# A bidirectional recurrent scan on one Trainium2 core: conditioning blocks, their PSUM bank, chunk tiles and squares moved

## Chip, cores and metric

The kernel runs on one core of one Trainium2 chip. The metric is the time of one execution on the device, in microseconds (us). The core has TensorE (matrix products), VectorE, ScalarE and GpSimd (element-wise work) and SyncE (here it only issues DMAs). In the rows they are called PE (PEld for its weight loads), DVE, ACT, POOL and SP. Each engine runs its own instructions in order.

## What is computed

One inference step of a trunk with two layers over 128 context tokens and 512 latent tokens of width 1024. Layer 0 mixes tokens by a delta-rule recurrence in both directions (16 heads of 64), layer 1 by neighbourhood attention; a squared-ReLU MLP of width 4096 follows each. Every sub-layer is modulated by shift, scale and gate from the conditioning vector (adaLN).

```python
def ada_mod(cond, w, b):
    m = jax.nn.silu(cond) @ w + b
    return jnp.split(m, 6, axis=-1)

def delta_rule_scan(r, w, k, v, kk, a, s0, reverse):
    def step(S, inp):
        r_t, w_t, k_t, v_t, kk_t, a_t = inp
        sa = jnp.einsum('bhvk,bhk->bhv', S, -kk_t)
        S_new = (S * w_t[:, :, None, :] + sa[..., None] * (kk_t * a_t)[:, :, None, :]
                 + v_t[..., None] * k_t[:, :, None, :]).astype(S.dtype)
        y = jnp.einsum('bhvk,bhk->bhv', S_new, r_t)
        return S_new, y
...
    y = (ys[0] + ys[1]).astype(jnp.float32)
    mean = jnp.mean(y, axis=-1, keepdims=True)
    var = jnp.mean(jnp.square(y - mean), axis=-1, keepdims=True)
    yn = ((y - mean) * lax.rsqrt(var + GN_EPS)).reshape(B, T, D) * ln_w + ln_b
```

## The kernel before

The stages follow one another: projections of layer 0 (to about 290 us), the values' product and the first preparations of the scan (to 400), the scan (400 to about 760), its output product (to about 875), the MLP of layer 0 (to 1347), layer 1's attention (to about 1715) and its MLP (to the end).

The recurrence is run in chunks of 32 tokens. A scan step n (five of them) takes one tile of 128 tokens in each direction d, and has four chunk steps e = 0 to 3. `chain_step` is one chunk in one direction: the product R of the state (tile GU) with the chunk tile C; its copy Rc by ScalarE; the product U with the inverse triangle TT; four copies of U back into GU by ScalarE (L1052); `state_update`, which makes the next state in the banks G (B in the rows) with work of VectorE (L1106, L1111) or ScalarE (L1108); and the output Y, evacuated by a ScalarE copy (L1069) or, where the other direction has been there, by a VectorE sum (L1067). R, U and Y of direction d use one PSUM bank, called A, in turn (one bank for each direction).

The chunk tiles of step n+1 are prepared beside the chunks of step n, in units of half a head group: GpSimd multiplies the loaded values into C and KB (`prep_elem`, L932, L933, L947), TensorE makes the products pp (`prep_group`), ScalarE copies the triangles to invA (L972) and the rest to C (L974), VectorE masks two parts of C (L977). A pp tile lies in one of two banks that take turns. Two units are prepared per chunk step. After the last unit of a step VectorE inverts 32 x 32 triangles by forward substitution (`invert`, L984 to L998; L993 and L996 are its 100 small operations), which gives the next TT.

Finished rows of Y go through `post_half` (head norm, gate): centring (L1139), the square (L1140, ScalarE), the variance (L1142, VectorE), on GpSimd or VectorE.

adaLN of a layer is 24 blocks of 256 columns. `ada_first` loads two pieces of 512 KB (adaraw, SyncE) and makes 8 products for 16 records on TensorE (L286; under the scan's `mm` L852), ScalarE copies the sums (L289). `ada_second` makes 2 products (4 records) with the copied sums (adasb), and VectorE adds the bias into mods (L300). Layer 0's blocks 8 to 23 run in the scan, one per chunk step of steps 0 to 3, with the second stage in U's bank of direction 1. Layer 1's 24 blocks run one at a time beside the weight products of the MLP of layer 0 (8), the attention layer (12) and the MLP of layer 1 (4).

In the scan TensorE's order is the order of the program text (`mm` ties each product to the one before). On the other engines a scheduler sets the order when the kernel is built, from its own estimate of times, with the marked copies first; at run time each engine keeps that order and waits.

Of the kernel before, what the change touches and what calls it, by code (L numbers as in the profile page):

```python
# [8 lines left out]
F32 = mybir.dt.float32  # L9
F32R = mybir.dt.float32r  # L10
I32 = mybir.dt.int32
AF = mybir.ActivationFunctionType
ALU = mybir.AluOpType
# [159 lines left out]
class K:  # L173
# [243 lines left out]

    def rest_begin(self, st):
        self.sqp = self.pool(st, "sqp", 2)
        self.ada1 = list(range(24))  # L420

    def pool(self, st, name, bufs, **k):
        return st.enter_context(self.tc.tile_pool(name=name, bufs=bufs, reuse_waits="tile", **k))
# [303 lines left out]

    def c_slots(self, pool, n, par):

        for i in range(n):  # L730
            c = pool.tile([P, 26, 64], F32, name=f"C{i}")
            self.nc.any.tensor_copy(c[:, 16:18, :].rearrange("p a x -> p (a x)"), self.cst("ident"))
            self.free[par].append(c)

    def scan_pools(self, st):
# [36 lines left out]

    def phase_scan(self, st):
        nc, tc = self.nc, self.tc
        if True:
            pool = lambda name, bufs, **k: self.pool(st, name, bufs, **k)
            self.yp = pool("yp", 4)
            adp = pool("adp", 2)
            one = pool("one", 1)
            self.ch = pool("ch", 1, space=PSUM)  # L780
            self.post = pool("post", 2)
            self.G = [self.ch.tile([P, 512], F32, name=f"B{d}").rearrange("p (a b v) -> p a b v", a=2, b=4) for d in range(2)]
            self.lnwb = one.tile([P, 2, 256], F32, name="lnwb")
            nc.scalar.dma_start(self.lnwb, self.A["lnwb"].rearrange("p (a x) -> p a x", a=2))
            self.cst2 = st.enter_context(ExitStack())
            self.c_slots(self.pool(self.cst2, "c2", 1), 4, 1)
            for d in range(2):
                self.gu[d].append(one.tile([P, 2, 2, 4, 64], F32, name=f"GU{d}1"))
                for h in range(2):
                    nc.gpsimd.memset(self.gu[d][1][64 - 64 * h:96 - 64 * h, h], 0.0)  # L790
            self.gi = [0, 0]
            self.yt = {}
            self.ydone = {}
            todo, running = [], []
            ada = [(0, b) for b in range(8, 24)]

            def ada_next():
                if ada:
                    pa = self.pp_tile()
                    pa = pa[:, :256]  # L800
                    self.ada_sums.append(self.ada_first(*ada.pop(0), adp, pa, self.mm))

            self.ada_sums = []
            done = {(0, 3): [(4, 0), (4, 1)], (3, 1): [(2, 0), (1, 1)], (3, 3): [(2, 1), (1, 0)],
                    (4, 1): [(3, 0), (0, 1)], (4, 3): [(3, 1), (0, 0)]}
            pend = None
            self.pin = True
            for n, ts in enumerate(self.steps):
                for e in range(4):
                    s0, s1 = (self.chain_step(ts, n, e, d) for d in range(2))  # L810
                    next(s0)
                    if pend:
                        for x in pend:
                            next(x)
                        if n == 4 and not self.late:
                            self.late_pools()
                        for t in done.get((n, e - 1) if e else (n - 1, 3), []):
                            todo.append(self.post_half(*t, n == 4 and t[0] % 3))
                    f = (0, 1, 1, 2)
                    k = self.fill(f[0])  # L820
                    next(s0)
                    k += self.fill(f[1])
                    ada_next()
                    k += self.fill(f[2])
                    next(s1)
                    next(s0)
                    next(s0)
                    next(s1)
                    k = self.fill(f[3])
                    if k:  # L830
                        next(s1)
                    pend = [s1] if k else [s1, s1]
                    for x in running:
                        next(x)
                    m = 2 if n == 4 else 1
                    running, todo = todo[:m], todo[m:]
                    for _ in range(2):
                        for x in running:
                            next(x)
            for x in pend:  # L840
                next(x)
            for x in running:
                next(x)
            todo += [self.post_half(*t, i) for i, t in enumerate(done[4, 3])]
            for _ in range(3):
                for x in todo:
                    next(x)
            self.wo_first(adp)

    def mm(self, *a, op=None, **k):  # L850
# [49 lines left out]
    def prep_elem(self, ts, hg, d, i):  # L900
# [32 lines left out]
                nc.gpsimd.tensor_tensor(rev(KB[:, :, :, 0]), v4(dd, 1, x), f_b, op=ALU.mult)  # L933
        f_at, f_rt = (ex(w, ww), inc(w, ww)) if d == 0 else (inc(wi, ww), ex(wi, ww))
        C = ts["C"][d, hg, ww] = self.free[ts["par"]].pop(0)
        for h in range(2):
            z = C[64 - 64 * h:P - 64 * h, 8 * h:8 * h + 8, :]
            if h:
                nc.scalar.activation(z.rearrange("p a b -> p (a b)"), self.cst("scan1")[64 - 64 * h:P - 64 * h, :512],
                                     AF.Copy, scale=0.0)  # L940
            else:
                nc.gpsimd.memset(z, 0.0)
        for s, f in ((0, f_at), (1, f_rt)):
            for h in range(2):
                hs = slice(64 * h, 64 * h + 64)
# [3 lines left out]
    def prep_group(self, ts, hg, d, i, e):  # L949

        nc = self.nc
        ww = (i, 1 - i)[d]
        KB, C = ts["KB", hg, d, i], ts["C"][d, hg, ww]
        if e == 0:
            self.pa = self.pp_tile()
        pa = self.pa
        pv = pa.rearrange("p (e q x) -> p e q x", e=2, q=4)
        for q in range(4):
            for h in range(2):
                n = 8 * h + 4 * e + q  # L960
                r = 64 - 64 * h
                self.mm(pv[r:r + 64, e, q, :], lhsT=KB[:, q, e].rearrange("p s t -> p (s t)"), rhs=C[:, n:17 + h:16 + h - n, :],
                        start=True, stop=True, tile_position=(0, r))
        if e == 0:
            return
        if "D" not in ts:
            ts["D"] = self.inv.tile([P, 2, 8, 2, 32], F32, name="invA")
        mask = self.cst(f"amask{d}").unsqueeze(1).broadcast_to([P, 8, 64])
        pn = pa.rearrange("p (n x) -> p n x", x=P)
        for h in range(2):  # L970
            for b in range(2):
                nc.scalar.copy(ts["D"][32 * (2 * h + b):32 * (2 * h + b) + 32, d, 4 * hg + 2 * ww:4 * hg + 2 * ww + 2],  # L972
                               pv[64 - 64 * h:96 - 64 * h, :, b:4:2, 0:32])
        nc.scalar.copy(C[:, 18:26, :], pn[:, :, 64:P])  # L974
        for h in range(2):
            o = slice(64 - 64 * h, P - 64 * h)
            nc.vector.tensor_tensor(C[o, 8 * h:8 * h + 8, :], pn[o, :, 0:64], mask[o], op=ALU.mult)  # L977
# [23 lines left out]
    def chain_step(self, ts, n, e, d):  # L1001
# [19 lines left out]
        C = [ts["C"][d, hg, ww] for hg in range(2)]  # L1021

        def state_product(s):
            ps = self.ch.tile([P, 512], F32, name=f"A{d}")[:, :256]
            for ph, pp, hp in idx:
                q = 2 * hp + pp
                i = 8 * hp + 4 * ee + 2 * (ph % 2) + pp
                self.mm(ps[32 * q:32 * q + 32, 64 * ph:64 * ph + 64], lhsT=C[ph // 2][:, i, 32 * s:32 * s + 32],
                        rhs=gu[:, hp, pp, ph, :], start=True, stop=True, tile_position=(0, 32 * q))
            return ps  # L1030

        R = state_product(0)
        with tc.high_priority():
            Rc = self.yp.tile([P, 256], F32, name="Rc", bufs=2)
            nc.scalar.copy(Rc, R)
        yield
        TT = ts["TT"]
        ut = self.ch.tile([P, 512], F32, name=f"A{d}")
        U = ut[:, :256]
        for ph, pp, hp in idx:  # L1040
            q = 2 * hp + pp
            o = slice(64 * ph, 64 * ph + 64)
            qs = slice(32 * q, 32 * q + 32)
            self.mm(U[qs, o], lhsT=TT[qs, d * 16 + ((ph // 2) * 4 + cq) * 2 + ph % 2, :],
                    rhs=Rc[qs, o], start=True, stop=True, tile_position=(32 * q, 32 * q))
        if self.ada_sums and d == 1:
            self.ada_second(*self.ada_sums.pop(0), ut[:, 256:260], self.mm)
        with tc.high_priority():
            for pp in range(2):
                for hp in range(2):  # L1050
# [5 lines left out]
            self.state_update(ts, n, e, d, gu, nx, C)  # L1056
        self.gi[d] += 1
        yield
        Y = state_product(1)
        tt = ts["tiles"][d]  # L1060
        with tc.high_priority():
            if tt not in self.yt:
# [5 lines left out]
            else:  # L1068
                nc.scalar.copy(yo, Y)  # L1069
                self.ydone[tt].add(cq)  # L1070
        if e % 2 == 1:
            self.free[ts["par"]] += [ts["C"].pop((d, hg, ww)) for hg in range(2)]
        yield

    def state_update(self, ts, n, e, d, gu, nx, C):
# [13 lines left out]
        for pp in range(2):  # L1089
            for ph in range(4):  # L1090
                for hp in range(2):
                    i = 18 + 4 * ee + 2 * (ph % 2) + pp
                    self.mm(G[hs(hp), pp, ph, :], lhsT=C[ph // 2][ho(hp), i, :], rhs=gu[ho(hp), hp, pp, ph, :],
                            start=False, stop=True, tile_position=(64 - 64 * hp, 64 * hp), skip_group_check=True)
        FC = ts["FC"]
# [18 lines left out]
    def post_half(self, tt, hb, on_dve):  # L1114
# [22 lines left out]
        nc.vector.tensor_scalar(sm, sm, 1.0 / 64, None, op0=ALU.mult)  # L1137
        bcast = lambda a: a.unsqueeze(2).broadcast_to([P, 8, 64])
        el.tensor_tensor(Yg, Yg, bcast(sm), op=ALU.subtract)  # L1139
        nc.scalar.activation(sq, Yg, AF.Square)  # L1140
        var = po.tile([P, 8], F32, name="yvar")
        nc.vector.tensor_reduce(var, sq, axis=AX.X, op=ALU.add)  # L1142
        nc.vector.tensor_scalar(var, var, 1.0 / 64, 64e-5, op0=ALU.mult, op1=ALU.add)
# [454 lines left out]
```

## Time and profile before

| | |
|---|---|
| median of 3 runs | 2232.8 us (2231.12 to 2234.78) |
| profiled execution | 2239.71 us |
| its span on the core | 2237.9 us |
| mean granted TensorE clock | 0.944 |
| TensorE busy | 2011.6 us (90%) |
| VectorE busy | 1169.5 us (52%) |
| ScalarE busy | 857.0 us (38%) |
| GpSimd busy | 455.1 us (20%) |
| TensorE's share of the chain that ended last | 74% |
| VectorE's share of it | 13% |

The span runs from the first to the last instruction of the core. The chain that ended last is followed back from the last instruction, at each step to what released it. A busy time is the sum of an engine's instructions; short TensorE records overlap, so their durations add up to more than the time they take together.

### The profile page before, as it was taken

What the parts mean: (1) busy time and instruction counts of PE and PEld (TensorE: products, weight loads), DVE (VectorE), ACT (ScalarE), POOL (GpSimd) and SP (SyncE); (2) the same over time, 40 slices, a digit from 0 to 9 for tenths busy, and PEclk for the clock granted to TensorE, in tenths of its full rate; (3) what the DMA queues carried; (4) which work ended last, traced back from release to release, by engine and by line L of the source; (5) the groups of instructions that cost most, each with busy time, mean ns of one, the idle gap of its engine ahead of it and who ended that gap; (6) DMA issues with size and microseconds to landing.
All of it is one profiled execution on the core that took longest, in us unless ns stands there. A gap on an engine that the chain in (4) does not pass through costs nothing.

```text
span 2237.9 us, 44938 instructions
## 1 busy us (share of the span) xinstructions
PE 2011.6 (90%) x18604; PEld 1827.3 (82%) x18604; DVE 1169.5 (52%) x2592; ACT 857.0 (38%) x1712; POOL 455.1 (20%) x553
## 2 busy tenths in 40 slices
PE   6999988757665569999999999999999999999999
PEld 3777777646554568999999998889677999999999
DVE  6656658387679755433333434433666633434342
ACT  4544553546553414313131323221576331313130
POOL 0001275656542411101010110000232110101010
PEclk8997999978787788999999999999899999999999
DMA  6455764545433464323232223343310232222221
GB/s 242 147 157 155 229 205 135 173 133 166 129 132 96 112 187 141 105 76 111 72 111 76 86 76 119 132 135 92 110 57 31 75 122 76 76 76 76 76 74 69
DMA packets 161037, 260.03 MB, mean 116 GB/s; under 512 B 46528, under 2 KB 102976, under 8 KB 160832
## 3 DMA queue, kind: packets, MB, share of 16 engines
q1 hardware_dynamic: 152224, 244.05, 35.2%
q10 hardware_dynamic: 8608, 13.11, 1.7%
q8 instruction: 146, 2.39, 0.4%
q14 instruction: 59, 0.48, 0.1%
HBM read 218.18 MB, written 37.35 MB: 114 GB/s over the span
## 4 chain that ended last, share of the span: by engine, by line
PE 74%; DVE 13%; DMA 5%; POOL 3%; issue 2%; ACT 2%; SPq 1%; DVEq 0%; ACTq 0%; POOLq 0%
PE psl L205 54%; PE psl L239 3%; DVE invX L996 2%; PE ps L1525 2%; DVE invT L993 2%; POOL C L947 2%; PE po L1562 2%; PE pp L852 2%; PE pt L1550 2%; DVE C L977 1%; PE pp L1219 1%; PE psl L1265 1%; PE psl L286 1%; DMA ld_s<-scr 1%; PE A L852 1%
## 5 line engine op out<-in xcount | busy, mean ns | idle before, releaser
L191 ACT CAST whi<-wraw 128x1024 fp32r<-128x1024 f32 x178 | 186.6, 1049 | 731.5 <-PE psl L205 701.9
L205 PE MATMUL psl<-xh,whi 128*128 128x320 f32 (+1 forms) x1696 | 414.6, 317 | 9.6 <-ACT xh L247 4.9
L205 PE MATMUL psl<-xl,whi 128*128 128x320 f32 (+1 forms) x1696 | 410.2, 314 | 1.2 <-DVE xl L248 1.2
L205 PE MATMUL psl<-xh,wlo 128*128 128x320 f32 (+1 forms) x1696 | 409.7, 314 | 0.4 <-DVE ta L592 0.4
L205 PEld LDWEIGHTS psl<-xh,whi 128*128 128x128 f32 x1696 | 291.4, 191 | 28.5 <-issue 8.7
L205 PEld LDWEIGHTS psl<-xl,whi 128*128 128x128 f32 x1696 | 292.5, 191 | 5.7 <-issue 3.2
L205 PEld LDWEIGHTS psl<-xh,wlo 128*128 128x128 f32 x1696 | 292.9, 191 | 2.6 <-issue 1.7
L1172 DVE SCALAR_TENSOR_TENSOR xres<-psl,mods,xres 128x320 f32<-128x320 f32 (+2 forms) x216 | 81.7, 434 | 305.1 <-PE psl L205 305.1
L1345 POOL TENSOR_TENSOR relu<-relu 128x640 f32<-128x640 f32 x64 | 80.2, 1255 | 773.9 <-ACT relu L1344 758.7
L205 PE MATMUL psl<-hhl,whi 128*128 128x320 f32 x1024 | 233.1, 308 | 0.0
L205 PE MATMUL psl<-hhh,wlo 128*128 128x320 f32 x1024 | 233.0, 308 | 0.0
L205 PE MATMUL psl<-hhh,whi 128*128 128x320 f32 x1024 | 232.9, 308 | 0.0
L193 DVE TENSOR_TENSOR wlo<-wraw,whi 128x1024 fp32r<-128x1024 f32 x178 | 218.6, 1229 | 11.6 <-ACT whi L191 10.9
L205 PEld LDWEIGHTS psl<-hhh,whi 128*128 128x128 f32 x1024 | 170.8, 188 | 0.4 <-issue 0.4
L205 PEld LDWEIGHTS psl<-hhh,wlo 128*128 128x128 f32 x1024 | 171.1, 188 | 0.0
L205 PEld LDWEIGHTS psl<-hhl,whi 128*128 128x128 f32 x1024 | 171.0, 188 | 0.0
L1302 DVE TENSOR_TENSOR relu<-psl,rms_b 128x320 f32<-128x320 f32 x128 | 60.8, 486 | 144.6 <-PE psl L205 144.0
L852 PE MATMUL pp<-C,KB 128*64 128x128 f32 x1280 | 100.6, 306 | 39.7 <-DVE C L977 16.7
L852 PEld LDWEIGHTS pp<-C,KB 128*64 128x64 f32 x1280 | 83.0, 154 | 54.1 <-issue 28.8
L248 DVE TENSOR_TENSOR hhl<-relu,hhh 128x640 fp32r<-128x640 f32 x64 | 53.4, 834 | 127.9 <-ACT hhh L247 127.7
L1052 ACT ACTIVATE GU<-A 32x256 f32<-32x256 f32 x160 | 60.0, 375 | 93.2 <-DVE mods L300 64.0
L977 DVE TENSOR_TENSOR C<-pp,cstsb 64x512 f32<-64x512 f32 x80 | 55.0, 688 | 69.1 <-ACT C L974 56.9
(299 smaller groups left out, 3393.2 us busy)
## 6 DMA issues: line engine op xcount, KB each, us to landing
wraw<-in_mlp_w SPq DMA_DIRECT2D x128, 512.0 KB, 3.5
adaraw<-in_ada_w SPq DMA_DIRECT2D x96, 512.0 KB, 4.9
ld_d<-scr SPq DMA_DIRECT2D x20, 512.0 KB, 4.5
ld_s<-scr SPq DMA_DIRECT2D x20, 512.0 KB, 3.7
bias<-in_bias SPq DMA_DIRECT2D x16, 384.0 KB, 3.7
scr<-ta SPq DMA_DIRECT2D x16, 325.0 KB, 3.5
wi<-scr SPq DMA_DIRECT2D x20, 260.0 KB, 4.6
scr<-bp SPq DMA_DIRECT2D x16, 320.0 KB, 4.5
```

Of the source, the lines that this page charges most:

```text
L191: nc.scalar.copy(hi, raw)
L193: nc.vector.tensor_tensor(lo, raw, hi.bitcast(F32), op=ALU.subtract)
L205: self.nc.tensor.matmul(ps[g][:, :e - c], lhsT=a[:, k, :], rhs=b[:, c:e], start=(k == 0 and j == 0), stop=(k == n - 1 and j == 2))
L239: nc.tensor.matmul(ps, lhsT=a[:, tc_], rhs=w, start=(k == 0 and j == 0), stop=(k == KT - 1 and j == 2))
L248: (lo_eng or nc.vector).tensor_tensor(xl, src, xh.bitcast(F32), op=ALU.subtract)
L852: r = (op or self.nc.tensor.matmul)(*a, **k)
L947: nc.gpsimd.tensor_tensor(rev(o) if s == 0 else o, v4(sh, s, ww)[hs], f[hs], op=ALU.mult)
L977: nc.vector.tensor_tensor(C[o, 8 * h:8 * h + 8, :], pn[o, :, 0:64], mask[o], op=ALU.mult)
L1052: nc.scalar.activation(gu[64 - 64 * hp:96 - 64 * hp, hp, pp].rearrange("p b v -> p (b v)"), U[32 * q:32 * q + 32, :], AF.Copy, scale=-0.5)
L1172: nc.vector.scalar_tensor_tensor(out[:, a:b], ps[g][:, o:o + b - a], gate[:, k, j:j + 1], x[:, a:b], op0=ALU.mult, op1=ALU.add)
L1302: nc.vector.tensor_tensor(t[:, c], ps[q][:, :HALF], rb[:, c], op=ALU.mult)
L1345: nc.gpsimd.tensor_tensor(t, t, t, op=ALU.mult)
```

## The change

Four things are changed. The list of adaLN blocks that the scan works off grows by layer 1's 24; a second block is taken per chunk step in step 0 and, but for e = 1, in steps 1 to 3, which makes 29 in the scan, 13 of them layer 1's. The remaining 11 blocks of layer 1 stay with the MLP of layer 0 (8) and the attention layer (3), so that 9 leave the attention layer and 4 the MLP of layer 1. The second stage of a block goes to Y's part of the cycle: into Y's bank, behind Y's evacuation, in both directions. A chunk tile C is no longer filled with zeros; the pp products read only the 64 rows that hold values, and an identity of one slot takes the place of one of two. The square of the head norm goes from ScalarE to the engine of the centring.

```diff
@@ c_slots
-            c = pool.tile([P, 26, 64], F32, name=f"C{i}")
-            self.nc.any.tensor_copy(c[:, 16:18, :].rearrange("p a x -> p (a x)"), self.cst("ident"))
+            c = pool.tile([P, 25, 64], F32, name=f"C{i}")
+            self.nc.vector.tensor_tensor(c[:, 16], ident[:, :64], ident[:, 64:], op=ALU.add)
@@ phase_scan
+        self.ada1 = list(range(24))
-            ada = [(0, b) for b in range(8, 24)]
+            ada = [(0, b) for b in range(8, 24)] + [(1, b) for b in self.ada1]
...
                     k += self.fill(f[1])
-                    ada_next()
+                    if n < 4:
+                        ada_next()
...
                     k = self.fill(f[3])
+                    if n == 0 or n < 4 and e != 1:
+                        ada_next()
...
+            self.ada1 = [b for _, b in ada]
             self.wo_first(adp)
@@ prep_elem
-        for h in range(2):
-            z = C[64 - 64 * h:P - 64 * h, 8 * h:8 * h + 8, :]
-            if h:
-                nc.scalar.activation(z.rearrange("p a b -> p (a b)"), self.cst("scan1")[64 - 64 * h:P - 64 * h, :512],
-                                     AF.Copy, scale=0.0)
-            else:
-                nc.gpsimd.memset(z, 0.0)
@@ prep_group
-                self.mm(pv[r:r + 64, e, q, :], lhsT=KB[:, q, e].rearrange("p s t -> p (s t)"), rhs=C[:, n:17 + h:16 + h - n, :],
-                        start=True, stop=True, tile_position=(0, r))
+                hs = slice(64 * h, 64 * h + 64)
+                self.mm(pv[r:r + 64, e, q, :], lhsT=KB[hs, q, e].rearrange("p s t -> p (s t)"), rhs=C[hs, n:17:16 - n, :],
+                        start=True, stop=True, tile_position=(64 * h, r))
@@ chain_step
-        if self.ada_sums and d == 1:
-            self.ada_second(*self.ada_sums.pop(0), ut[:, 256:260], self.mm)
...
-        Y = state_product(1)
+        pa, Y = state_product(1)
...
                 nc.scalar.copy(yo, Y)
                 self.ydone[tt].add(cq)
+            if self.ada_sums:
+                self.ada_second(*self.ada_sums.pop(0), pa[:, 256:260], self.mm)
@@ post_half
-        nc.scalar.activation(sq, Yg, AF.Square)
+        el.tensor_tensor(sq, Yg, Yg, op=ALU.mult)
```

The change also moves instructions where the diff shows nothing. Three places follow, as the built kernels have them. A row reads line, operation, output<-inputs, shape, and how many like it; the line numbers of the kernel after are a few off (L976, L1064, L1105, L1110 and L997 there are L977, L1067, L1106, L1111 and L998 before). What an instruction waits for stands in brackets where it is shown.

VectorE in step 0, chunk steps 2 and 3. Before, these rows stand inside the inversion for step 1 (invT and invX are its operations):

```order
L977 TENSOR_TENSOR C_2652<-pp_4841,cstsb 64x512
L993 TENSOR_TENSOR invT_4407<-invX 128x98
L977 TENSOR_TENSOR C_2652<-pp_4841,cstsb 64x512
L996 TENSOR_TENSOR invX<-invX,invT_4406 128x15x10
L1106 TENSOR_TENSOR GU_2637<-B_3879,FC 64x512 x2
L996 TENSOR_TENSOR invX<-invX,invT_4407 128x14x7
L1067 TENSOR_TENSOR Y<-Y,A_4920 128x256
L993 TENSOR_TENSOR invT_4406<-invX 128x140
L300 TENSOR_TENSOR mods_96<-A_4938,parsb 128x4
L1111 TENSOR_TENSOR B_3879<-B_3879,FC 128x512
```

After, from the last operation of the same inversion on (L995; L997 delivers TT):

```order
L995 TENSOR_TENSOR invX<-invX,invT_4388 128x10
L997 STREAM_TRANSPOSE TT<-invX 128x32x32
L976 TENSOR_TENSOR C_2656<-pp_4735,cstsb 64x512 x2
L921 SCALAR_TENSOR_TENSOR wi<-cstsb,wi 128x520
L1064 TENSOR_TENSOR Y<-Y,A_4813 128x256
L300 TENSOR_TENSOR mods_96<-A_4813,parsb 128x4
L976 TENSOR_TENSOR C_2652<-pp_4855,cstsb 64x512 x2
L1105 TENSOR_TENSOR GU_2637<-B_3855,FC 64x512 x2
L1110 TENSOR_TENSOR B_3855<-B_3855,FC 128x512
L1064 TENSOR_TENSOR Y<-Y,A_4934 128x256
L300 TENSOR_TENSOR mods_96<-A_4934,parsb 128x4
L976 TENSOR_TENSOR C_2660<-pp_5001,cstsb 64x512 x2
```

The masks of C, the sums of Y and the additions for GU and B that stood between the inversion's operations stand behind TT; of the eight masks (L977) of the two chunk steps two are still inside.

TensorE in a chunk step of step 1. Before, from Y of direction 0 (the product A<-GU,C) over U of direction 1 (A<-Rc,TT) to the next unit's pp:

```order
L852 MATMUL A_5918<-GU_3894,C_2669 32x64 [waits PE_49]
L852 MATMUL A_5918<-GU_3894,C_2669 32x64 x7
L852 MATMUL A_5918<-GU_3894,C_3888 32x64 x8
L852 MATMUL A_5936<-Rc,TT 32x64 [waits Activation_49]
L852 MATMUL A_5936<-Rc,TT 32x64 x15
L852 MATMUL A_5936<-cstsb,adasb 128x2 x2
L852 MATMUL pp_5960<-C_3886,KB 64x128 [waits DVE_49,Pool_49]
```

After, the same stretch of a chunk step:

```order
L857 MATMUL A_6492<-GU_3870,C_2648 32x64 [waits PE_49]
L857 MATMUL A_6492<-GU_3870,C_2648 32x64 x7
L857 MATMUL A_6492<-GU_3870,C_2650 32x64 x8
L857 MATMUL A_6492<-cstsb,adasb 128x2 [waits Activation_49]
L857 MATMUL A_6492<-cstsb,adasb 128x2
L857 MATMUL A_6514<-Rc,TT 32x64 [waits PE_49]
L857 MATMUL A_6514<-Rc,TT 32x64 x15
L857 MATMUL pp_6535<-C_3864,KB 64x128 [waits DVE_49,Pool_49]
```

The second stage (cstsb,adasb) stood behind U and waited for nothing; it stands behind Y, waits for Y's copy by ScalarE, and U stands behind it.

ScalarE beside that, from the copy of R to the four copies of U of direction 1 (GU<-A). Before, in step 1:

```order
L1035 COPY Rc<-A_5881 128x256 [waits PE_49]
L1108 COPY GU_2637<-B_3879 64x512 [waits PE_49]
L1108 COPY GU_2637<-B_3879 64x512
L1069 COPY Y<-A_5918 128x256 [waits PE_49]
L917 ACTIVATE w<-wi 128x520 [waits DVE_49]
L1052 ACTIVATE GU_3897<-A_5936 32x256 [waits DVE_49]
L1052 ACTIVATE GU_3897<-A_5936 32x256 x3
```

After, at the same place of the first chunk step of step 1:

```order
L1035 COPY Rc<-A_5485 128x256 [waits PE_49,Activation_49]
L1066 COPY Y<-A_5523 128x256 [waits PE_49]
L922 ACTIVATE w<-wi 128x520 [waits DVE_49,Pool_49]
L923 ACTIVATE wi<-wi 128x520 [waits Activation_49]
L1049 ACTIVATE GU_2638<-A_5544 32x256 [waits PE_49]
L1049 ACTIVATE GU_2638<-A_5544 32x256 x3
```

The copies of U waited for VectorE, which reads the second stage out of U's bank; they wait for TensorE alone.

## Rows read from the trace of the kernel before

**Rows 1.** busy tenths of TensorE, 40 equal slices of the span (page)

```profile
PE   6999988757665569999999999999999999999999
```

**Rows 2.** by window: length; busy of PE, PEld, DVE, ACT, POOL; clock, DMA, GB/s

```profile
443.00:495.00 52.00, 25.14 (x646) 20.15 (x648) 50.99 (x138) 23.64 (x59) 29.65 (x45) 0.79 0.45 138
482.00:495.00 13.00, 0.25 (x12) 0.28 (x16) 12.85 (x44) 1.90 (x3) 6.07 (x9) 0.50 0.18 61
495.00:527.00 32.00, 28.06 (x724) 21.57 (x715) 12.93 (x26) 21.87 (x58) 18.05 (x26) 0.91 0.47 149
527.00:580.00 53.00, 30.70 (x660) 25.11 (x664) 52.29 (x139) 21.95 (x57) 33.12 (x44) 0.70 0.49 142
580.00:611.00 31.00, 27.25 (x728) 22.09 (x723) 12.12 (x18) 22.27 (x59) 14.79 (x23) 0.90 0.46 146
611.00:653.00 42.00, 24.90 (x644) 20.71 (x644) 40.42 (x120) 19.91 (x54) 23.06 (x28) 0.84 0.33 106
685.00:727.00 42.00, 22.30 (x544) 18.06 (x544) 41.41 (x148) 12.13 (x27) 11.09 (x9) 0.70 0.32 91
```

**Rows 3.** groups of instructions, VectorE, 443 to 495 us: busy us, mean ns

```profile
L996 DVE TENSOR_TENSOR invX<-invX,invT 128x108 f32<-128x108 f32 (+31 forms) x50 | 17.8, 379 | 0.3
L993 DVE TENSOR_TENSOR invT<-invX 128x20 f32<-128x20 f32 (+31 forms) x50 | 15.7, 337 | 0.3
L977 DVE TENSOR_TENSOR C<-pp,cstsb 64x512 f32<-64x512 f32 x9 | 6.2, 687 | 0.2
```

**Rows 4.** waits, 400 to 760 us: us in total, times, longest

```profile
ACT GU L1052 <- DVE mods L300: 64.0, 15, 13.2
...
PE A L852 <- DVE rsq_t L262: 19.3, 1, 19.3
...
PE A L852 <- ACT Rc L1035: 14.8, 14, 2.8
```

**Rows 5.** timeline of TensorE, 590 to 611 us: start, us, records, idle before

```profile
595.40 0.65 PE L852 MATMUL A<-Rc,TT 32*32 32x64 f32 x32 [1.11 <-ACT Rc L1035]
...
598.00 1.09 PE L852 MATMUL pp<-C,KB 128*64 128x128 f32 x16
...
599.03 0.65 PE L852 MATMUL A<-GU,C 128*32 128x64 f32 x32
...
599.61 1.15 PE L852 MATMUL B<-GU,C 64*64 64x64 f32 x32
...
609.53 0.65 PE L852 MATMUL A<-Rc,TT 32*32 32x64 f32 x32 [1.32 <-ACT Rc L1035]
```

**Rows 6.** chain that ended last, attention layer: start, us, what

```profile
1388.82 1.00 PE psl L286 x16
...
1393.92 0.54 PE psl L296 x4
```

**Rows 7.** the same chain, second MLP

```profile
1833.67 0.34 PE psl L296 x4
```

**Rows 8.** groups of instructions, all engines, 400 to 760 us

```profile
L852 PE MATMUL pp<-adaraw,condp 128*32 128x256 f32 x256 | 22.2, 470 | 3.0 <-DVE C L977 2.0 <-issue 0.8
...
L852 PE MATMUL A<-cstsb,adasb 128*128 128x2 f32 x64 | 9.7, 256 | 0.0
...
L942 POOL MEMSET C<- 64x512 f32 x28 | 14.6, 523 | 5.1 <-PE A L852 4.8
...
L1139 POOL TENSOR_TENSOR Y<-Y,ysum 128x512 f32<-128x512 f32 x5 | 5.2, 1045 | 59.1 <-DVE ysum L1137 59.0
```

**Rows 9.** chain that ended last, end of the chain stretch before 527 us

```profile
520.11 0.17 DVE mods L300
...
520.30 0.37 ACT GU L1052
...
523.52 1.23 DVE invA L984
```

**Rows 10.** the same chain, ahead of the scan, 286 to 325 us

```profile
306.37 2.86 POOL C L942 x6
```

More of the change, by code (lines that the diff above doesn't have):

```diff
@@ L419, in rest_begin @@
         self.sqp = self.pool(st, "sqp", 2)
-        self.ada1 = list(range(24))
     def pool(self, st, name, bufs, **k):
@@ L728, in c_slots @@
     def c_slots(self, pool, n, par):
+        ident = self.cst("ident")
         for i in range(n):
-            c = pool.tile([P, 26, 64], F32, name=f"C{i}")
-            self.nc.any.tensor_copy(c[:, 16:18, :].rearrange("p a x -> p (a x)"), self.cst("ident"))
+            c = pool.tile([P, 25, 64], F32, name=f"C{i}")
+            self.nc.vector.tensor_tensor(c[:, 16], ident[:, :64], ident[:, 64:], op=ALU.add)
             self.free[par].append(c)
@@ L973, in prep_group @@
                                pv[64 - 64 * h:96 - 64 * h, :, b:4:2, 0:32])
-        nc.scalar.copy(C[:, 18:26, :], pn[:, :, 64:P])
+        nc.scalar.copy(C[:, 17:25, :], pn[:, :, 64:P])
         for h in range(2):
@@ L1023, in state_product @@
         def state_product(s):
-            ps = self.ch.tile([P, 512], F32, name=f"A{d}")[:, :256]
+            pa = self.ch.tile([P, 512], F32, name=f"A{d}")
+            ps = pa[:, :256]
             for ph, pp, hp in idx:
@@ L1029, in state_product @@
                         rhs=gu[:, hp, pp, ph, :], start=True, stop=True, tile_position=(0, 32 * q))
-            return ps
-        R = state_product(0)
+            return pa, ps
+        _, R = state_product(0)
         with tc.high_priority():
@@ L1037, in chain_step @@
         TT = ts["TT"]
-        ut = self.ch.tile([P, 512], F32, name=f"A{d}")
-        U = ut[:, :256]
+        U = self.ch.tile([P, 512], F32, name=f"A{d}")[:, :256]
         for ph, pp, hp in idx:
@@ L1091, in state_update @@
                 for hp in range(2):
-                    i = 18 + 4 * ee + 2 * (ph % 2) + pp
+                    i = 17 + 4 * ee + 2 * (ph % 2) + pp
                     self.mm(G[hs(hp), pp, ph, :], lhsT=C[ph // 2][ho(hp), i, :], rhs=gu[ho(hp), hp, pp, ph, :],
```

## Prediction

> **What bounds the kernel now.** I read the busy tenths of TensorE first: full from about 840 us to the end, with a trough of fives to eights from 280 to 840 [rows 1]. In the full part a removed TensorE instruction is time saved. Most of the trough is the recurrent scan, so I cut 443 to 727 into windows at the points where VectorE's load changes [rows 2]. Two kinds of stretch alternate. In an *inversion stretch* VectorE is busy 50.99 of 52, 52.29 of 53, 40.42 of 42, 41.41 of 42 us: it solves the next step's triangles, 100 small operations (17.8 and 15.7 us of the first [rows 3]) mixed with work for the running step's chunks e=2, e=3. TensorE has 22 to 31 us of work there and ends up waiting for the result TT, 19.3 us the first time (the row names rsq_t, the first operation behind TT on VectorE) [rows 4]. In a *chain stretch* (32 and 31 us, the third like them) VectorE is busy 12 to 13 us, TensorE 27 to 28: chunks e=0 and e=1 run as a chain R, copy, U, copy, G, Y through three engines, at nearly TensorE's pace. From one U (595.40) to the U of the next chunk (609.53) are 14.1 us [rows 5]. So the scan's time is inversion plus chain, and what matters is how many chunks run beside an inversion and how many behind it.
>
> **The change, part by part.**
>
> *Thirteen adaLN blocks leave layer 1.* In the attention layer a block costs the chain 1.00 us (16 products) and 0.54 us (4 products) [rows 6], in the second MLP 0.34 for the latter [rows 7]. Nine of the first and four of the second: 9 x 1.54 + 4 x 1.34 = 19.2 us. Part of each 4-product piece is hand-over that stays, so I take **-18**. The engine there is full, no other cover. Their 26 loads of 512 KB leave those stages too, where nothing waits for them.
>
> *The same blocks in the scan.* 16 blocks now take 22.2 us of first-stage and 9.7 us of second-stage products [rows 8], 2.0 each; without the cold clock in part of the first stage, 1.0 as in the layers [rows 6], about 1.7. Of the 13 added, about seven stand where no inversion covers them (e=3 and e=0 of steps that follow one another, and one of step 0's four): 7 x 1.7 = **+12**; all 13 exposed would be +26, none 0. The two loads of each go through SyncE's queue, ahead of the chunk's v loads and the next group's loads; the present 32 share it. I add nothing for that and keep 3 us for the range.
>
> *Second stage in Y's bank.* It goes, and so does a good thing. Before, the U copy on ScalarE of direction 1 waits until VectorE has read the modulation out of the same bank: 64.0 us in 15 waits [rows 4]. Most lies in inversion stretches where nobody asks for it; at the end of a chain stretch it is on the chain that starts the next inversion: mods at 520.11, then four U copies from 520.30, then copies of the last triangles, then the mask of them at 523.52 [rows 9]. The U copies would come about 3.5 us earlier; that start is the same in two of the four inversions (the first follows loads, the fourth the variance of the head norm): **-7** (0 to -14). In exchange each of 29 second stages now waits, on the in-order TensorE, for Y's evacuation by ScalarE or VectorE; behind it queue the next U or R, and the next R of that direction waits for the mods. The nearest row is the round trip TensorE-ScalarE-TensorE for Rc: 14.8 us in 14 waits, 1.06 each [rows 4]. ScalarE copies Rc first and Y directly after, so the new wait covers the old one in part; I take 0.6 for 13 exposed: **+8** (4 to 14).
>
> *Chunk tiles without zeros.* GpSimd loses its zero fills, 14.6 us in 28 [rows 8], ScalarE as many. Only where GpSimd leads the chain does that count: before step 0, six fills in a row, 2.86 us, lie on the chain that ended last [rows 10]. **-3** (0 to -5). The products pp become 64-row tiles. Now 16 records of pp take 1.09 us; the products G, already 64 x 64 tiles on the same diagonal, take 1.15 for 32 records of half the columns [rows 5], so 16 records of full width may cost up to 1.15: 0 to +0.06 per half group, at most +3 in the scan; I take 0.
>
> For that there is a rule that speaks against the change. The rows say: the U products (32 x 32, four row tiles, one bank) take 0.65 us for 32 records, and the R and Y products, column tiles over all rows, 0.65 for the same records [rows 5]; row tiles in one bank cost nothing extra here. The Trainium skill, "TensorEngine Tiling (Array Packing)", section "Gotcha 1: PSUM Pressure", says that different row tiles cannot access the same PSUM bank simultaneously. By it the new pp pairs, both in one bank, would follow one another. The trace disagrees with it for U; what it would give is the last rival.
>
> *Squares.* Seven go to GpSimd at about the price of the centring beside them, 1.05 us [rows 8], three to VectorE. In the order two of the variances now stand in VectorE's queue ahead of the inversion's first operation. With VectorE slowed a little beside GpSimd's arithmetic I take **+1** (-1 to +4).
>
> *What moves by itself: VectorE's order.* This is the largest term and in no line of the diff. In the first inversion of the scan only two of eight chunk masks (0.69 us each [rows 3]) and one of four Y sums stay; the rest stands behind TT. By the counts of the order and such prices the four inversions lose about 9.5, 9, 1.5 and 6 us: **-26**. But TensorE's order is fixed by hand, and a group's products wait for the tile that the mask before must empty. So it stops in e=2 or at its end, and e=3 follows TT. Pairs of masks behind TT and up to the next inversion's start: seven, six, six, where four, four, five stood, at two pairs per chunk. Counting where in the inversion the last inner mask stands, about 1, 0.7, 0.2 and 0.3 chunks more run uncovered, 2.2 in all. One chunk is the 14.1 us above, less about 0.8 that the freed U copies give: 2.2 x 13.3 = **+29** (15 to 43). The waits for TT vanish within this: TensorE stands idle inside the inversion instead, held by a mask.
>
> Sum: -18 + 12 - 7 + 8 - 3 + 1 - 26 + 29 = **-4 us**. The profiled execution took 2239.7 (span 2237.9), so about 2236 for one like it; it lay 6.9 above the median of 2232.8, and I take the difference over: **2229**. A measurement of this kernel tells about 0.2%, 4.5 us, from no change.
>
> **The rivals.**
>
> *A chunk too many behind each TT* (slower). VectorE's queue holds TensorE earlier than I counted, half a chunk more for each of the first three inversions: 3 x 6.7 = +20, net +16: **2249**. It decides from the moment when TensorE stops more than 20 us before TT with e=2 unfinished. For it: the order puts up to 60 rows of the inversion between neighbouring masks where it had 10 to 25. Against: the chain stretches leave VectorE over half idle, so e=3 itself runs at full pace there.
>
> *The inversions win* (faster). If e=2 and most of e=3 still fit beside them, only 1.2 chunks move: -13, net -17: **2216**. For it: TensorE now idles for its last 13 to 20 us there (0.25 of 13 us busy [rows 2]), so there is room; fewer products in GpSimd's arithmetic beside a shorter inversion would also speed VectorE. Against: the masks inside are few, and order is order.
>
> *The row tiles exclude each other.* Sixteen records 2.18 instead of 1.09, 56 halves in the scan, some 36 uncovered: +39, **2268**. The U products speak against it.
>
> **How the numbers follow.** Main case 0.41, its own range 2222 to 2236; slower rival 0.27; faster rival 0.28; row tiles 0.04. Within the main case somewhat under half lies under 2228.3 and somewhat under half within 0.2%. Faster: 0.28 + 0.18 = 0.46; same 0.20 + 0.04 from the edges of the others = 0.24; slower 0.30. For eight in ten the range takes both near rivals with most of their spread (loads, stalls, squares): 2211 to 2252.
>
> **What would show it.** In the profile after: the attention layer and second MLP together shorter by 17 to 19 us with no first-stage product in the latter; inversions of 39 to 44 us instead of 50; TensorE idle in their second half, waiting for a mask or a Y sum and no longer for TT; 40 us and more from TT to the next inversion; U copies that wait for TensorE alone; new waits of 0.5 to 1 us of a second stage for Y. A pp group of 16 records over 1.3 us at full clock would prove the row-tile rival. The forecast is wrong if the stretch from 400 to 760 us grows by over 30 us or does not grow at all.

## The result

The changed kernel takes 2301.9 us (median of 5 runs, 2293.9 to 2304.4) against 2232.9 of the kernel before: 1.030 times as long, 95% interval 1.0277 to 1.0323. The forecast was 2229, range 2211 to 2252. It was wrong in sign and outside its range.

The profiled execution's span is 2292.1 us, 54 more than before. Where they lie shows in the page's tenths, the answer to [rows 1]: the trough (slices of seven and less behind the first full ones) is ten slices long instead of eight, a slice being some 57 us, and no emptier, about six tenths on average in both.

```profile
span 2292.1 us, 44817 instructions
...
PE   6999897566667566999999999999999999999999
```

The windows, cut at the starts and ends of three inversions (columns as in [rows 2]):

```profile
446.00:476.00 30.00, 13.72 (x251) 10.91 (x254) 28.45 (x112) 7.58 (x19) 7.32 (x12) 0.73 0.33 107
476.00:560.00 84.00, 54.80 (x1220) 41.76 (x1220) 35.33 (x69) 35.52 (x94) 42.06 (x58) 0.83 0.49 155
560.00:593.00 33.00, 17.25 (x278) 13.38 (x282) 32.09 (x115) 9.49 (x24) 12.43 (x13) 0.71 0.40 137
593.00:666.00 73.00, 52.66 (x1182) 41.12 (x1178) 23.17 (x35) 32.49 (x87) 29.83 (x43) 0.79 0.44 139
666.00:700.00 34.00, 15.68 (x355) 12.85 (x349) 31.10 (x111) 11.63 (x30) 12.93 (x16) 0.73 0.41 129
700.00:757.00 57.00, 44.03 (x1069) 34.40 (x1066) 23.97 (x50) 23.78 (x67) 16.48 (x21) 0.86 0.46 155
```

The inversions became shorter than I had said: 30, 33, 34 us, where 49, 50 and 37 stood from the first operation to TT. The stretches from TT to the next inversion became 83, 73 and 57 us, where 35, 34 and 36 stood. In the first of them TensorE is busy 54.8 of 84 us and VectorE 35: neither is the bound. So the chunks behind TT do not run at TensorE's pace. Who holds whom is in the waits of 400 to 850 us (total, times, longest), the answer to [rows 4]:

```profile
DVE C L976 <- ACT C L973: 87.5, 17, 7.3
...
ACT w L922 <- DVE wi L921: 63.2, 6, 14.8
...
PE A L857 <- DVE Y L1064: 45.8, 11, 8.6
DVE wi L921 <- DMA wi<-scr: 44.7, 9, 14.7
...
PEld pp L857 <- DMA adaraw<-in_ada_w: 40.7, 14, 7.8
...
PE A L857 <- ACT Y L1066: 37.3, 17, 11.4
```

The kernel before had most of these waits too, but shorter, and none of pp for adaraw (400 to 760 us, the window of [rows 4]):

```profile
DVE C L977 <- ACT C L974: 42.6, 8, 10.8
...
ACT w L917 <- DVE wi L916: 20.1, 5, 7.8
...
PE A L852 <- DVE Y L1067: 15.1, 4, 8.5
...
DVE wi L916 <- DMA wi<-scr: 10.6, 3, 4.7
```

The loads wi (the decay sums of the next units) and adaraw, VectorE's sum of wi, ScalarE's exponential w behind it: engines now wait longer for the preparation of the next units. The wait of U's copies for the mods, 64.0 us in [rows 4], is gone; the list after the change has none.

Behind the scan the change did what it says. The attention layer's first product comes at 1426.5 us instead of 1350.0, so everything up to there takes 76 us more. From the first TT to the last alone it is 68 us more (398.9 against 330.7), where the prediction named a growth of over 30 as a sign of its being wrong. From the attention layer to the end the kernel takes 22 us less, and the attention layer still shows the two pieces of [rows 6] where a block is left:

```profile
1454.80 1.00 PE psl L286 x16
1459.88 0.54 PE psl L296 x4
```

### The profile page after: what moved, and what is told of

Same layout as the page of the kernel before. It is cut to its first block, busy times and chain, and to the rows that moved or that the text cites. A ratio compares the mean times of both kernels' runs of the same rounds, so it can differ in the third digit from the quotient of the medians.

```text
span 2292.1 us, 44817 instructions
## 1 busy us (share of the span) xinstructions
PE 2022.2 (88%) x18604; PEld 1834.8 (80%) x18604; DVE 1158.1 (51%) x2605; ACT 831.5 (36%) x1652; POOL 441.0 (19%) x520
## 4 chain that ended last, share of the span: by engine, by line
PE 72%; DVE 10%; DMA 7%; POOL 5%; issue 3%; ACT 2%; SPq 1%; DVEq 0%; POOLq 0%; ACTq 0%
PE psl L205 52%; POOL C L945 3%; PE psl L239 3%; PE ps L1524 2%; PE pp L857 2%; PE po L1561 2%; DMA adaraw<-in_ada_w 2%; DMA wi<-scr 2%; DVE invT L992 2%; DVE invX L995 2%; PE pt L1549 2%; PE A L857 2%; PE pp L1218 1%; PE psl L1264 1%; DMA ld_s<-scr 1%
## 5 line engine op out<-in xcount | busy, mean ns | idle before, releaser
L205 PE MATMUL psl<-xh,whi 128*128 128x320 f32 (+1 forms) x1696 | 408.6, 314 | 9.8 <-ACT xh L247 5.4
L857 PE MATMUL pp<-C,KB 64*64 64x128 f32 x1280 | 106.3, 319 | 21.4 <-DVE C L976 9.3
L857 PEld LDWEIGHTS pp<-C,KB 64*64 64x64 f32 x1280 | 88.3, 160 | 37.4 <-issue 16.3
L976 DVE TENSOR_TENSOR C<-pp,cstsb 64x512 f32<-64x512 f32 x80 | 55.1, 689 | 105.1 <-ACT C L973 104.0
L857 PE MATMUL A<-cstsb,adasb 128*128 128x2 f32 x116 | 21.6, 290 | 80.3 <-DVE Y L1064 38.0
```

Of the source, the lines that this page charges most:

```text
L205: self.nc.tensor.matmul(ps[g][:, :e - c], lhsT=a[:, k, :], rhs=b[:, c:e], start=(k == 0 and j == 0), stop=(k == n - 1 and j == 2))
L857: r = (op or self.nc.tensor.matmul)(*a, **k)
```

## The experiments

Each is timed beside the kernel before on the same chip, which there took 2238 to 2242 us; a number in brackets is the ratio to it with its interval. Loss means the difference to that kernel before, 69 us for the changed kernel in the result above. What an edit to the changed kernel gives is the difference of two losses, because the kernel before itself took 5 to 9 us less beside the changed kernel than in these runs.

**First, parts undone one at a time.** The first of the runs takes out the 13 blocks (`ada` has layer 0's 16 alone, the second `ada_next` goes).

> The changed kernel without its first part: the scan works off only layer 0's 16 blocks, one per chunk step, and layer 1's 24 stay in the layers; second stage in Y's bank, chunk tiles without zeros and squares off ScalarE remain. Theory L (the second block per chunk step: its two 512 KB loads find both buffers taken, come late for TensorE and hold SyncE's queue ahead of the wi and ld loads): the scan's growth of some 78 us goes, the 18 to 24 us won behind it go too: 2225 to 2245 us. Theory Y (every second stage waits for Y's evacuation and holds TensorE): 16 of 29 such waits stay, 2265 to 2285. Theory R (64-row tiles of pp exclude each other in one bank): 2300 or more.

2280.6 us (1.020, 1.016 to 1.023). Not L: without the 13 blocks 39 us of the loss stay, so taking them out gives 30. The time lies in Y's range.

The second run keeps the blocks and takes out their loads alone:

```diff
-                raw = pool.tile([P, 4, 256], F32, name="adaraw")
-                nc.sync.dma_start(raw, self.A["ada_w"][l, blk, :, 4 * h:4 * h + 4])
+            own = not (l == 1 and mm)
+            if own:
+                raw = ...
...
-                rhs=raw[:, c, :]
+                rhs=raw[:, c, :] if own else self.cst("scan1")[:, :256]
```

> The changed kernel, but the 13 blocks of layer 1 in the scan multiply a constant that is already there and load nothing (their modulation is therefore not the reference's); all products, copies and second stages stay. L: TensorE no longer waits for these loads and SyncE's queue is free: 2235 to 2255 us, and no wait of pp for adaraw of over 3 us in all. Y: nothing changes in the waits behind Y, 2290 to 2305. R: 2295 to 2305.

2286.5 us (1.022, 1.019 to 1.025), a loss of 45: the 26 loads account for some 24 us, no more, and the time is in no theory's range. Layer 0's loads, which stay, still hold pp for 22 us; that part of my expectation was careless.

> The changed kernel with the second stage back in U's bank, behind U, now in both directions (29 of them); all else as changed. L: the loads are as late as before, 2290 to 2310 us. Y: the waits of the second stage for Y (83 us in all in the profile of the changed kernel) go and do not come back elsewhere, 2240 to 2270, less what the U copies lose by waiting for the mods.

2287.3 us (1.023, 1.020 to 1.026), a loss of 45: 24 us, again a part, and short of Y's range.

> The changed kernel with the zero-filled chunk tiles and the products over all 128 rows put back; all else as changed. R: pp goes back to 1.09 us per 16 records and the scan gains some 40 us: 2255 to 2270. L and Y: the zero fills come back on GpSimd and ScalarE, 2300 to 2312 us.

2254.1 us (1.005, 1.002 to 1.008), a loss of 12. So 57 of the 69 us hang on the chunk tiles, about what R had asked for. But R's mechanism is not there: pp takes 1.09 us for 16 records in either form. The first row is of the changed kernel (64-row tiles), the second of the one with the zeros back (timeline of TensorE):

```profile
600.45 1.09 PE L857 MATMUL pp<-C,KB 64*64 64x128 f32 x16
```

```profile
598.66 1.09 PE L857 MATMUL pp<-C,KB 128*64 128x128 f32 x16
```

What differs between the two, besides fills and products, is the order that the scheduler builds: 6, 6, 4 masks inside the three inversions instead of 2, 4, 4. Hence theory O.

**The form of the products alone.** To the kernel before, nothing but this:

```diff
-                self.mm(pv[r:r + 64, e, q, :], lhsT=KB[:, q, e]..., rhs=C[:, n:17 + h:16 + h - n, :], ..., tile_position=(0, r))
+                self.mm(pv[r:r + 64, e, q, :], lhsT=KB[hs, q, e]..., rhs=C[hs, n:17 + h:16 + h - n, :], ..., tile_position=(64 * h, r))
```

> The kernel before with one edit: pp multiplies the 64 rows that hold values (tiles of 64 rows) instead of all 128; the zero fills stay, all else is the kernel before. In the built order the chunk masks inside the three inversions fall from 8, 8, 6 to 4, 4, 4. Theory O (VectorE's order: masks put behind TT hold TensorE, whose own order is fixed): slower than before by 20 to 45 us, with pp at 1.09 us per 16 records as before, shorter inversions and longer stretches from TT to the next inversion. Theory R (the products themselves are slower): pp over 1.3 us. Theory L (loads of the second block): no change, within 5 us of before.

2288.1 us (1.021, 1.019 to 1.024): one edit that removes no instruction and adds none costs 49 us, a little over what O had asked for.

> The kernel before with the 13 blocks of layer 1 in the scan and nothing else of the change: second stage in U's bank, in both directions. The order keeps 8, 8, 8 masks inside the inversions. O: the scan grows by the blocks' own products and waits only, 10 to 25 us, and 18 to 24 go behind it: within 10 us of before, 2223 to 2243. L: the second block's loads hold SyncE and TensorE, the scan grows by 50 to 80 us: 2265 to 2295.

2241.4 us (1.001, 0.9996 to 1.002), in O's range. The 13 blocks by themselves are free here: what they win behind the scan they cost in it. pp waits 6.3 us for their loads there, not 33.8 as in the changed kernel.

**Is it the masks?** The change's VectorE order, with the masks of chunks e=2 and e=3 put back between the inversion's operations by hand (`invert` yields after each column, each mask is tied to the operation before it):

```diff
+    def inv_next(self):
+        to = self.inv_to.pop(0) if self.inv_to else 99
+        for s in self.invg:
+            if s == to:
+                return
...
```

> The changed kernel, all four parts, with VectorE's order of masks and inversion written out by hand: the four pairs of masks of chunks e=2 and e=3 stand behind 8, 24, 48 and 72 of the inversion's 100 operations, as many as before the change inside. No work differs from the changed kernel. O: the scan gets back most of its 78 us: 2215 to 2250. L: the loads still come late and now hold VectorE too, 2290 to 2320.

> As the one with masks put inside by hand, but with only layer 0's 16 blocks in the scan: the difference to it is the price of the 13 blocks when VectorE's order is the same. O: 2225 to 2245, so within 15 us of the one with 29 blocks. L: 40 to 70 us faster than the one with 29 blocks.

2303.3 us (1.028, 1.026 to 1.031) and 2297.7 (1.026, 1.024 to 1.028): nothing gained with 29 blocks, and with 16 a loss of 59 us where the scheduler's order had 39. The first time is in L's range, but L wanted 40 to 70 us between the two, and they are 6 apart. So the masks' place, which my term for VectorE's order went by, is not the cause by itself. Now the inversion waits: 68 us, VectorE busy 41.0 of them (the first inversion of the run with 29 blocks, and its waits of 400 to 800 us):

```profile
455.00:523.00 68.00, 34.07 (x716) 26.97 (x708) 41.01 (x125) 20.92 (x54) 26.06 (x38) 0.75 0.43 140
```

```profile
DVE C L996 <- ACT C L993: 93.1, 21, 8.0
```

**Order without any difference in the work.** The order of VectorE, ScalarE, GpSimd and SyncE within the scan is taken from one build and written into another, instruction by instruction:

```diff
+            for seq in ORDER.values():
+                for a, b in zip(seq, seq[1:]):
+                    tc.add_manual_dep(nc.get_inst_by_name(f"I-{b}"), f"I-{a}", ...)
```

> The kernel before with pp as tiles of 64 rows, and on VectorE, ScalarE, GpSimd and SyncE the order of the kernel before, written out instruction by instruction for the scan. It differs from the kernel before by the products alone, and from the one with 64 rows and the scheduler's order (2288 us) by order alone. Theory O (the form of the products only changes the order that the scheduler builds on all engines, and that order costs the time): within 6 us of before. Theory H (the form itself costs time on the chip, in the products or through what they collide with): 2275 to 2295 us.

> The counterpart: the kernel before, products over 128 rows as they were, with the order on VectorE, ScalarE, GpSimd and SyncE that the scheduler builds for the 64-row form. No operation differs from the kernel before. O: 2275 to 2300 us. H: within 6 us of before.

2244.2 us (1.0035, 1.002 to 1.005) and 2271.5 (1.016, 1.013 to 1.018). The new products in the old order lose 5 of the 49 us; the old products in the new order, the same work to the last operation, lose 32. The first is as O said, the second 4 us short of its range and far from H's 6. This shows that the order costs most of the time. (The form adds 5 in the old order and 17 in the new; the products' busy time is 100.0 against 100.6 us, so it is not in them, and I leave it open.) The windows of the two, 64 rows in the old order first, then 128 rows in the new one, each an inversion and the stretch behind it:

```profile
445.00:495.00 50.00, 24.45 (x632) 19.65 (x624) 49.08 (x134) 23.14 (x57) 29.16 (x44) 0.80 0.47 144
495.00:531.00 36.00, 29.97 (x724) 23.51 (x724) 13.92 (x29) 22.68 (x60) 20.03 (x27) 0.85 0.40 123
```

```profile
449.00:487.00 38.00, 20.14 (x390) 15.53 (x388) 36.39 (x116) 13.82 (x37) 15.10 (x22) 0.73 0.38 120
487.00:543.00 56.00, 41.78 (x984) 33.01 (x976) 25.06 (x45) 31.93 (x80) 33.30 (x48) 0.82 0.42 128
```

In the second, the chain that ended last shows for one place what a chunk behind TT waits for (start, us, what):

```profile
502.11 0.66 POOL KB L937
502.79 0.34 SPq L916
...
507.26 5.59 DMA wi<-scr
...
512.94 1.25 DVE wi L920
514.22 0.65 ACT w L921
514.89 0.64 ACT wi L922
515.55 0.26 ACT invA L976
...
517.20 0.28 ACT Rc L1039
517.53 1.90 PE A L856 x36
```

GpSimd frees a buffer, SyncE works off nine issues until the load wi is out, 5.6 us of transfer, VectorE's sum, two exponentials; and the copy Rc, on which TensorE's next U hangs, stands behind them on ScalarE. A step has four such runs, one for each load of wi. In the old order VectorE's sums of three of them lie beside the inversion, which takes 50 us anyway (454.8, 463.4 and 492.4 us, with TT at 494.1), and one behind it; in the new order two and two (460.4 and 483.4, TT at 484.5, then 512.9 and 528.5).

**The change in such an order.** The same writing-in for the changed kernel, with the order that the scheduler builds for it when pp is written over 128 rows:

> The changed kernel, all four parts, with the order on the four engines that the scheduler builds when pp is written over 128 rows (the order has 6, 6, 4 masks inside the inversions instead of 2, 4, 4). O: the 64-row form's share, 40 to 50 us, comes back: 2240 to 2262, like the one with the zero fills put back (2254). H: 2290 to 2305.

> The changed kernel without the 13 blocks, again with the order built for pp over 128 rows (6, 8, 8 masks inside). O: 2225 to 2245 us, against 2281 with the scheduler's own order. H: 2275 to 2285.

2252.6 us (1.006, 1.004 to 1.008) and 2250.8 (1.005, 1.003 to 1.007): 55 us come back in the first, which is in O's range, and 27 in the second, which is 6 us above it. With such an order the 13 blocks again cost what they win.

> The kernel before with one part of the change, chunk tiles without zeros and 64-row products, and the order that the scheduler builds when the products are written over 128 rows (8, 8, 8 masks inside). If the zero fills' 14.6 us on GpSimd and 17 on ScalarE lie on the chain where I saw them, 2228 to 2236 us on the scale of 2239 for the kernel before (3 to 10 us faster); if other waits take their place, 2236 to 2248.

> As the one with the chunk tiles alone, with the squares off ScalarE too; second stage in U's bank (both directions), 16 blocks in the scan, order built for 128 rows. If the squares on GpSimd and VectorE cost the 12 us: 10 or more above the one with the chunk tiles alone. If Y's bank costs them: within 4 us of the one with the chunk tiles alone, and some 10 us under the same with the second stage in Y's bank (2251).

> Chunk tiles without zeros and the 13 blocks, second stage in U's bank in both directions, squares on ScalarE as before, order built for 128 rows (8, 8, 8 masks inside). The candidate for a version that beats both: the layers gain 18 us and the scan pays for the blocks what it did in the kernel before with 13 blocks (about 20): 2228 to 2245 us.

> The changed kernel with the second stage in U's bank instead of Y's (both directions), order built for 128 rows (8, 6, 8 masks inside). Against the one with Y's bank and such an order (2252.5): if the waits behind Y cost, 5 to 15 us less, 2237 to 2247; if not, 2248 to 2258.

2237.7 us (1.0005, 0.999 to 1.002), 2251.4 (1.007, 1.005 to 1.009), 2246.1 (1.004, 1.003 to 1.006) and 2241.7 (1.003, 1.0004 to 1.005). The third, the candidate, is 1 us over the range I gave it. The zero fills' absence wins nothing. The squares seem to cost 14 us in the second, but the fourth has the squares too, 13 blocks more, and is 10 faster. Each build has an order of its own, and I take it that these differ by some 10 us among themselves: the 13 blocks cost 3 us in the kernel before, 2 with Y's bank, 8 without the squares, and -10 between the second and the fourth. The parts' own prices cannot be had below that. Y's bank against U's costs 24 us (changed order), 10 (order for 128 rows, 29 stages) and nothing (16 stages). No version beat the kernel before.

**Which engine's order?** Both from the kernel before with the new order, one engine given back its old one:

> The kernel before with the order built for 64 rows on VectorE, GpSimd and SyncE, and its own old order on ScalarE; products over 128 rows, no operation differs. Theory S (ScalarE's exponential w stands ahead of the chain's copies and waits for a load): the waits of Rc behind w go, 2235 to 2252 us. Theory D (VectorE's order, masks and sums behind TT): 2262 to 2280. Theory Q (SyncE issues the loads late): 2262 to 2280.

> As that, but SyncE gets its old order back and ScalarE keeps the new one. Q: the wi loads are issued earlier, 2235 to 2252 us. S and D: 2262 to 2280.

2286.6 us (1.022, 1.019 to 1.025) and 2296.1 (1.025, 1.020 to 1.030): both slower than with the new order throughout (2271.5). S and Q, which asked for 2235 to 2252, fall; D's 2262 to 2280 is missed too. With the old order on ScalarE the wait of w for wi shrinks from 62.8 us to 27.2, but others grow (waits of 400 to 800 us):

```profile
ACT GU L1056 <- DVE mods L300: 96.6, 16, 18.0
...
PE pp L856 <- DVE C L981: 43.1, 8, 13.4
```

With the new order on all four (400 to 770 us) they were:

```profile
ACT GU L1056 <- DVE mods L300: 54.5, 15, 15.2
...
PE pp L856 <- DVE C L981: 16.5, 5, 5.2
```

So an old order on one engine, put beside new ones on the others, brings waits of its own, and these two runs cannot say which engine's order carries the loss. The old order on VectorE alone or on GpSimd alone was not tried; the masks put back by hand speak against VectorE's masks alone. What is shown is that the four orders together cost the time.

## Why the prediction was wrong, step by step

*Blocks leaving layer 1*, -18: right; -22 from the attention layer on.

*Zero fills*, -3: the part alone gave nothing (2237.7 against 2238.2). The first TT does come 9 us earlier in the trace of the changed kernel, but in the other traces without the fills it comes anywhere from 8 us earlier to no earlier at all. *pp's form*, 0 to +3 on TensorE: right for the products (100.6 us with 128 rows, 100.0 with 64 rows in the old order). The last rival, that row tiles exclude each other, fell: two 64-row tiles in one bank take the 1.09 us that two column tiles took. The Trainium skill, "TensorEngine Tiling (Array Packing)", section "Gotcha 1: PSUM Pressure", says that different row tiles cannot access the same PSUM bank simultaneously; for these products, which write different partitions of the bank, the traces show no cost of it.

*Blocks in the scan*, +12, loads at nothing: mis-sized. Taking them out of the changed kernel gave 30 us, net of the some 20 that they win behind it, so they cost some 50 there; in a good order some 20. I had put SyncE's queue at zero; the loads alone are worth 24 us in the changed kernel.

*Second stage in Y's bank*, +8 -7: together +1, measured 24, 10 and nothing by the order it stands in. The waits for Y that I put at 0.6 us each are 2.2 (17 for ScalarE's copy) and 4.2 us (11 for VectorE's sum), in part off the chain. The freed U copies were no help that could be seen.

*Squares*, +1: somewhere between nothing and 14 us; the builds' own orders hide it.

*VectorE's order*, -26 +29: this is the step that failed. What moved I counted somewhat low. By the U products, two to a chunk, the three stretches behind TT hold 3.5, 3.5 and 3 chunks where each held 2.5, and the fourth inversion covers half a chunk less: three chunks became uncovered and not 2.2. The inversions shrank twice as much as I said, from 175 us (four of them) to 124. Some 23 of these 51 us are not work that moved but the 100 small operations themselves, 138 us before and 115 after; in the first inversion, against [rows 3] (VectorE, 446 to 480 us):

```profile
L992 DVE TENSOR_TENSOR invT<-invX 128x20 f32<-128x20 f32 (+31 forms) x50 | 12.5, 275 | 0.4
L995 DVE TENSOR_TENSOR invX<-invX,invT 128x108 f32<-128x108 f32 (+31 forms) x50 | 12.2, 275 | 0.3
```

GpSimd is busy 7 us beside this inversion where it was busy 29. This much of the faster rival came true.

The price of a chunk behind TT was wrong. I took 13.3 us, from the time from one U to the next in a stretch of the kernel before [rows 5]. But there three of the four sums of wi of a step stand beside the inversion and one behind it; in the changed kernel it is one and three (timeline of VectorE, 443 to 562 us, before and after; other rows left out):

```profile
453.21 1.23 DVE L916 TENSOR_TENSOR_SCAN wi<-cstsb,wi 128x520 f32<-128x520 f32 x1
461.86 1.24 DVE L916 TENSOR_TENSOR_SCAN wi<-cstsb,wi 128x520 f32<-128x520 f32 x1
490.98 1.23 DVE L916 TENSOR_TENSOR_SCAN wi<-cstsb,wi 128x520 f32<-128x520 f32 x1
492.67 1.93 DVE L998 STREAM_TRANSPOSE TT<-invX 128x1024 f32<-128x1024 f32 x1
514.12 1.24 DVE L916 TENSOR_TENSOR_SCAN wi<-cstsb,wi 128x520 f32<-128x520 f32 x1 [3.58 <-DMA wi<-scr]
```

```profile
458.46 1.24 DVE L921 TENSOR_TENSOR_SCAN wi<-cstsb,wi 128x520 f32<-128x520 f32 x1 [0.78 <-DMA wi<-scr]
476.83 1.99 DVE L997 STREAM_TRANSPOSE TT<-invX 128x1024 f32<-128x1024 f32 x1
483.34 1.24 DVE L921 TENSOR_TENSOR_SCAN wi<-cstsb,wi 128x520 f32<-128x520 f32 x1 [3.11 <-DMA wi<-scr]
519.56 1.24 DVE L921 TENSOR_TENSOR_SCAN wi<-cstsb,wi 128x520 f32<-128x520 f32 x1 [3.26 <-DMA wi<-scr]
538.39 1.24 DVE L921 TENSOR_TENSOR_SCAN wi<-cstsb,wi 128x520 f32<-128x520 f32 x1 [3.77 <-DMA wi<-scr]
```

The stretches after take 57 to 83 us, 19 to 24 us a chunk, where they took about 14. Together they grew by 107 us, the blocks' products and waits included; three chunks at my price would have been 40. With the order alone changed (128 rows in the new order, no operation different) the four inversions lose 28 us and the three stretches gain 54. A moved chunk takes its preparation along, and that runs through the queues in turn: DMA 5 to 6 us, VectorE, ScalarE twice, GpSimd eight products, TensorE, ScalarE, VectorE. That this preparation makes the price is read from the chain and the waits; no run took it away by itself. The slower rival ("a chunk too many") had the direction and some of the count; its mechanism, masks alone, fell with the hand-placed masks.

And the reason for the move I did not see at all. I read the order as a consequence of all four parts together. For the larger part it is one edit, the form of pp: with it alone the inversions of the kernel before hold 4, 4, 4 masks instead of 8, 8, 6, and without it the other parts leave 6, 6, 4. Why the scheduler builds another order for the 64-row form was not looked into; on the chip the products take the same time.

## What to carry to other kernels

When a scheduler orders the engines, compare the order it builds for each edit by itself before pricing the edit's work: here an edit that left the products' own time as it was cost 49 us, and writing the old order into the new kernel took a loop of manual dependencies. A step that moves from beside a long operation to behind it is priced by all that has to happen for it since its last cover, not by the spacing of such steps where they were prepared ahead. And where every engine works off its queue in order, mending one queue need not help: the masks put back on VectorE and the old orders on ScalarE and on SyncE, each by itself, gained nothing.

## What the runs showed of the hardware

Two 64 x 64 tiles of TensorE on the array's diagonal that write different partitions of one bank run as fast (1.09 us for 16 records at a granted clock of 1.00) as two 128 x 64 column tiles.

A small operation of VectorE's inversion takes about twice as long while GpSimd works beside it: over the 54 shapes that occur both ways in the trace of the kernel before, 0.53 us against 0.27 on average.
